# Sparse attention from a written list of steps, shifted copies in one transfer, two squares summed on the matrix engine

## The chip, the cores and the metric

One core of a Trainium2 chip runs the whole program. The metric is device time in microseconds (us) of one execution; the kernel before has a median of 1078.66 us over 3 runs (1078.24 to 1082.45). The engines are PE (matrix engine; PEld is its weight load), DVE (VectorE), ACT (ScalarE), POOL (GpSimd) and SP, which issues the weight loads. Each runs its own instructions in their order and waits on semaphores.

## What is computed

The input is 256 rows of 1024 channels in float32. A first block (mLSTM and window attention, cross attention, feed-forward) is followed by two layers: a conformer convolution with feed-forward, and a sparse attention (NSA) with feed-forward. Three parts of it matter here, cut from the reference:

```python
# every norm: the row's mean square
y = xf * rsqrt(mean(xf * xf, axis=-1) + eps)
# conformer: depthwise convolution over time, 31 taps, on u = a * sigmoid(g)
u[t, c] = sum_j w[j, c] * u[t - 30 + j, c] + b[c]
# NSA, 16 heads of 64 channels, 4 key groups: three branches and a gate for each
o = g[0] * softmax(q k_cmp) v_cmp + g[1] * softmax(q k_slc) v_slc + g[2] * softmax(q k_win) v_win
```

With 256 rows every block is chosen and the window covers all, so the last two branches are plain causal attention, with keys and values of their own.

## The kernel before

Activations lie as 8 tiles of 128 channels x 256 rows. A float32 product is made of three products of float32r halves: each weight chunk of 128x1024 is loaded raw, rounded by ACT (L232, "hi"), its rest taken by DVE (L233, "lo"), and `mm3` (L260 to L262) makes the three products. Weights come through SP in one order for the whole program, four raw chunks ahead.

A norm (`norm`, L478) handles the 8 tiles one by one: DVE adds the residual (L527), ACT rounds (L409), DVE takes the rest (L410), ACT squares (L470), POOL adds the squares of tiles 0 to 6 into one tile (`rowsums`, L500 and L503), and PE multiplies that tile and the last square with ones (L508) into the bank `zb`. Meanwhile PE makes the first product of the next layer, step by step behind the tiles. There are six such sums; four of them have this form.

The conformer (L1050) adds named steps to a `Plan`, each with an engine, an assumed length and what it needs; `Plan.run` puts the steps in order of assumed time and that order is fixed for PE, DVE, ACT and POOL. The first 16 or 20 taps of the convolution are done by PE: for each of 8 tiles, step `w` (L1150) writes the padded rows to DRAM (`cz`), step `c` (L1158) reads them back four times, shifted by 0 to 3 rows, into four groups of 32 partitions (`crp`), in four transfers; step `t` (L1167) multiplies it with the taps in tiles of 32 columns, four beside each other. All of these transfers are issued by POOL, in order; `c` waits until the write of `w` has landed. The other taps are done by DVE (L1197). When all 8 tiles are done, PE sums them and their squares (L1243), the statistics follow (L1255 and on), and the projection starts.

Sparse attention (L1379) is a set of generators: each unit (a projection, an attention unit of one head pair and branch, a finish) yields between its parts, `NSA_AT` has a time for each, and `timed` emits the parts in that order; from there the compiler's scheduler orders each engine. An attention unit (16 of them) makes scores (L1592, L1595; 64 rows, two heads beside each other), maxima (DVE, L819), exponentials (ACT, L1603, L1605), transposes the probabilities (L827 to L829, copied out by ACT, L831), and multiplies them with the values: `out[queries, 64] = pT^T v`, six products (L1620 to L1622). DVE scales the result by gate and denominator (L1627), POOL adds the two branches (L1633), PE adds the compressed branch (L1642, DVE L1644), and the sum is transposed back (L1648) and split into hi and lo (L414, L415) for the output projection. The rotations (L1448 to L1453) are done by DVE.

Of the kernel before, what the change touches and what calls it, by code (L numbers as in the profile page):

```python
# [9 lines left out]
F32 = mybir.dt.float32  # L10
# [3 lines left out]
ALU = mybir.AluOpType  # L14
# [31 lines left out]
NSA_AT = [  # L46
# [46 lines left out]
class Plan:  # L93
# [9 lines left out]
    def add(self, name, eng, us, fn, need=(), rank=0, at=0.0, lag=0.0):  # L103

        self.names[name] = len(self.steps)
        self.steps.append((name, eng, us, fn, list(need), rank, at, lag))

    def run(self):
        free = dict.fromkeys(self.ENGINES, 0.0)
        done, left, order = {}, list(range(len(self.steps))), []  # L110
        while left:
            best = None
            for i in left:
                name, eng, us, fn, need, rank, at, lag = self.steps[i]
                if any(n not in done for n in need):
                    continue
                t = max([at, free[eng]] + [done[n] + ((0.11 if eng == "dv" else 0.0) if self.steps[self.names[n]][1] == eng else 0.15)
                                           for n in need])
                if best is None or (t, rank, i) < best[0:3]:
                    best = (t, rank, i)  # L120
            t, _, i = best
            name, eng, us, fn, need, rank, at, lag = self.steps[i]
            free[eng] = t + us
            done[name] = t + us + lag
            left.remove(i)
            order.append((t, i))
        self.order = sorted(order)
        with self.tc.manual_schedule(engines={e for e in self.ENGINES.values() if e}):
            for _, i in self.order:
                self.steps[i][3]()  # L130


class Net:
# [70 lines left out]
    def parts(self):  # L204

        while True:
            self.run_ahead(stop=self.coming())
# [282 lines left out]
    def rowsums(self, n):  # L490

        def run():
            acc = None
            for m in range(n - 1):
                sq = yield
                if m == 0:
# [9 lines left out]
            for tt in range(NT):  # L506
                for src in (acc, sq):
# [316 lines left out]
    def pT3(self, p):  # L824
# [228 lines left out]
    def conformer(self, first, pool):  # L1053
# [54 lines left out]
        for m in range(KT):  # L1108
# [43 lines left out]
            @step(f"c{m}", "gp", 2.3 if m < NREP else 2.9, [f"w{m}"] + ([f"t{m - NREP}"] if m >= NREP else []), 0, lag=3.5)  # L1152
            def _(m=m):
# [225 lines left out]
    def nsa(self, first, pool):  # L1379
# [25 lines left out]
        have = set()  # L1405

        def need(*keys):
            while not have.issuperset(keys):
                yield
# [5 lines left out]
        def vals(c, put, key):  # L1415
            b = self.lin2A(self.chunk("n_in", c), xx)
            yield
            for tt in range(NT):
                nc.scalar.mul(put(tt), b[tt].rearrange("p (g d) -> p g d", g=4), rc[:, tt : tt + 1])
            have.add(key)  # L1420
            yield

        def heads(c, gi, dst, key):

            b = b0 if ("n_in", c) in FIRST else self.lin2A(self.chunk("n_in", c), xx)
            yield
            b4 = [t.rearrange("p (h d) -> p h d", h=4) for t in b]
            sq = pool.tile([P, NT, 4, dh], F32, name="nsq", tag="nsq", bufs=1)
            for tt in range(NT):
                nc.scalar.activation(sq[:, tt], b4[tt], AF.Square)  # L1430
            ss = pool.tile([P, NT, 4], F32, name="nss", tag="nss", bufs=2)
            nc.vector.tensor_reduce(ss, sq, axis=AX.X, op=ALU.add)

            nc.vector.tensor_scalar(ss, ss, 1.0 / dh, None, op0=ALU.mult)
            nc.vector.tensor_tensor(ss, ss, r2.unsqueeze(2).to_broadcast([P, NT, 4]), op=ALU.add)
            rs = self.rsqrt(ss.rearrange("p t h -> p (t h)"), NT * 4, "h").rearrange("p (t h) -> p t h", t=2)
            yield
            y = pool.tile([P, NT, 4, dh], F32, name="ny", tag="ny", bufs=2)
            for tt in range(NT):
                nc.vector.tensor_tensor(y[:, tt], b4[tt], rs[:, tt].unsqueeze(2).to_broadcast([P, 4, dh]), op=ALU.mult)  # L1440
            z = kvc[:, :, :, 0:dh] if dst is None else y
            nc.vector.tensor_tensor(z.rearrange("p t h d -> p (t h) d"), y.rearrange("p t h d -> p (t h) d"),
                                    gain[:, gi, :].unsqueeze(1).to_broadcast([P, 8, dh]), op=ALU.mult)
            rt = pool.tile([P, 4, NT, 4, 8], F32, name="rot", tag="rot", bufs=2)
            cos = self.cs[:, :, 0, :].unsqueeze(2).to_broadcast([P, NT, 4, 8])
            sin = self.cs[:, :, 1, :].unsqueeze(2).to_broadcast([P, NT, 4, 8])
            x1, x2 = z[:, :, :, 0:8], z[:, :, :, 8:16]
            nc.vector.tensor_tensor(rt[:, 0], x1, cos, op=ALU.mult)  # L1448
            nc.vector.tensor_tensor(rt[:, 1], x2, sin, op=ALU.mult)
            nc.vector.tensor_tensor(rt[:, 2], x2, cos, op=ALU.mult)  # L1450
            nc.vector.tensor_tensor(rt[:, 3], x1, sin, op=ALU.mult)
            nc.vector.tensor_tensor(x1, rt[:, 0], rt[:, 1], op=ALU.subtract)
            nc.vector.tensor_tensor(x2, rt[:, 2], rt[:, 3], op=ALU.add)  # L1453
            if dst is None:
                have.add(key)
            yield
            if dst is not None:
                have.add(key)
                yf = y.rearrange("p t h d -> p t (h d)")
                tposes([(yf[:, 0, i * P : i * P + P], yf[:, 1, i * P : i * P + P]) for i in range(2)], dst)  # L1460
                yield

        def tposes(srcs, dst):
# [4 lines left out]
            nc.scalar.copy(dst, bt[:, 0 : len(srcs) * S])  # L1468
# [14 lines left out]
        def compress():  # L1483
            yield from need("kc", "vc")
            for g in range(0, G, 2):
                tposes([(kvc[:, 0, g + i, :], kvc[:, 1, g + i, :]) for i in range(2)], kvT[:, g : g + 2, :])
            yield
            bh = self.bank("bh")
            for hf in range(2):
                w1 = [r.rearrange("p (l e) -> p l e", l=8) for r in self.chunk("cmp_w1", hf)]  # L1490
                for i in range(16):
                    l = 16 * hf + i

                    nc.tensor.matmul(bh[:, 0:75].rearrange("p (g n) -> p g n", g=5), w1[i // 8][:, i % 8, :],  # L1494
                                     kvT[:, :, l : l + 225 : 16], start=(l == 0), stop=(l == 31))
            hb = pool.tile([P, 1], F32, name="hb")
            hx = pool.tile([P, 60], F32, name="hx")
            nc.vector.tensor_scalar(hb, bh[:, 60:61], self.col("b1", 0), None, op0=ALU.add)
            nc.vector.tensor_scalar(hx, bh[:, 0:60], hb, None, op0=ALU.add)
            yield  # L1500
            h2 = pool.tile([P, 60], F32, name="h2")
            gp = nc.gpsimd
            gp.tensor_tensor(h2, hx, hx, op=ALU.mult)
# [386 lines left out]
```

## Time and profile before

| | |
|---|---|
| median of 3 runs | 1078.66 us |
| profiled execution, its own time | 1083.75 us |
| its span, first to last instruction | 1082.0 us |
| PE busy, DVE busy, ACT busy, POOL busy | 98%, 73%, 56%, 12% of the span |
| mean granted clock of PE | 0.990 |
| sparse attention | about 737 to 887 us |
| conformer convolution, to its statistics | about 441 to 512 us |

Busy time of PE is not work at its peak: matmuls overlap, so a matmul shown with 0.28 us may start 0.12 us after the one before. For PE the distance from one start to the next is read. A float32 matmul that is not split stands as two records, so a count of 4 is two instructions. In the groups, "idle before" is the engine's idle time ahead of the instruction, with what ended it. The granted clock has two levels, shown as 1.0 (2.4 GHz) and 0.5 (1.2 GHz).

### The profile page before, as it was taken

What the parts mean: (1) busy time and instruction counts of PE and PEld (TensorE: products, weight loads), DVE (VectorE), ACT (ScalarE), POOL (GpSimd) and SP (SyncE); (2) the same over time, 40 slices, a digit from 0 to 9 for tenths busy, and PEclk for the clock granted to TensorE, in tenths of its full rate; (3) what the DMA queues carried; (4) which work ended last, traced back from release to release, by engine and by line L of the source; (5) the groups of instructions that cost most, each with busy time, mean ns of one, the idle gap of its engine ahead of it and who ended that gap; (6) DMA issues with size and microseconds to landing.
All of it is one profiled execution on the core that took longest, in us unless ns stands there. A gap on an engine that the chain in (4) does not pass through costs nothing.

```text
span 1082.0 us, 19870 instructions
## 1 busy us (share of the span) xinstructions
PE 1062.6 (98%) x7550; PEld 973.2 (90%) x7550; DVE 786.7 (73%) x1645; ACT 604.2 (56%) x1134; POOL 127.5 (12%) x335
## 2 busy tenths in 40 slices
PE   9999999999999999998999999999999999999998
PEld 8999999999999988984988888889998998888887
DVE  5886667757888865687988778665668657777763
ACT  7675556556666644422766666444466755666530
POOL 1020003002000000334030000013332112000000
PEclk8999999999999999998999999999999999999999
DMA  8654444434555665486555556655073035556670
GB/s 260 214 168 144 143 132 156 156 118 157 194 195 185 206 182 171 145 213 178 186 190 187 189 185 211 191 183 160 27 223 109 2 118 173 185 190 188 184 210 20
DMA packets 54711, 179.34 MB, mean 166 GB/s; under 512 B 9176, under 2 KB 11096, under 8 KB 54616
## 3 DMA queue, kind: packets, MB, share of 16 engines
q1 hardware_dynamic: 52056, 170.14, 49.5%
q0 software_dynamic: 2560, 7.95, 2.8%
q8 instruction: 59, 0.97, 0.4%
q14 instruction: 36, 0.29, 0.1%
HBM read 175.88 MB, written 2.17 MB: 165 GB/s over the span
## 4 chain that ended last, share of the span: by engine, by line
PE 84%; DVE 5%; DMA 5%; POOL 2%; ACT 2%; issue 2%; SPq 0%; ACTq 0%; POOLq 0%
PE pb L268 29%; PE pb L269 15%; PE pb L260 10%; PE pb L261 10%; PE pb L262 10%; DMA cz<-cuz 3%; POOL crp L1158 1%; DVE wpr L233 1%; DVE xx L410 1%; ACT wpr L232 1%; PE bh L1494 1%; DVE xres L527 1%; PE bt L1167 1%; PE pb L317 1%; DMA wraw<-in_n_out_dram 1%
## 5 line engine op out<-in xcount | busy, mean ns | idle before, releaser
L233 DVE TENSOR_TENSOR wpr<-wraw,wpr 128x1024 fp32r<-128x1024 f32 (+1 forms) x300 | 361.4, 1208 | 161.3 <-ACT wpr L232 159.0
L232 ACT CAST wpr<-wraw 128x1024 fp32r<-128x1024 f32 (+1 forms) x300 | 309.3, 1034 | 190.9 <-PE pb L269 98.0
L268 PE MATMUL pb<-xx,wpr 128*128 128x512 f32 x840 | 294.1, 393 | 0.0
L269 PE MATMUL pb<-xx,wpr 128*128 128x256 f32 x840 | 235.4, 280 | 0.0
L268 PEld LDWEIGHTS pb<-xx,wpr 128*128 128x128 f32 x840 | 158.4, 189 | 33.9
L268 PE MATMUL pb<-fhs,wpr 128*128 128x512 f32 x528 | 186.0, 394 | 0.0
L269 PEld LDWEIGHTS pb<-xx,wpr 128*128 128x128 f32 x840 | 158.5, 189 | 0.0
L269 PE MATMUL pb<-fhs,wpr 128*128 128x256 f32 x528 | 147.3, 279 | 0.0
L260 PE MATMUL pb<-xx,wpr 128*128 128x256 f32 x456 | 130.8, 288 | 0.0
L261 PE MATMUL pb<-xx,wpr 128*128 128x256 f32 x456 | 130.2, 286 | 0.0
L262 PE MATMUL pb<-xx,wpr 128*128 128x256 f32 x456 | 129.3, 284 | 0.0
L268 PEld LDWEIGHTS pb<-fhs,wpr 128*128 128x128 f32 x528 | 99.0, 187 | 23.1
L269 PEld LDWEIGHTS pb<-fhs,wpr 128*128 128x128 f32 x528 | 99.0, 187 | 0.0
L260 PEld LDWEIGHTS pb<-xx,wpr 128*128 128x128 f32 x456 | 87.4, 192 | 1.4
L261 PEld LDWEIGHTS pb<-xx,wpr 128*128 128x128 f32 x456 | 87.8, 193 | 0.9
L262 PEld LDWEIGHTS pb<-xx,wpr 128*128 128x128 f32 x456 | 87.7, 192 | 0.0
L260 PE MATMUL pb<-yy,wpr 128*128 128x256 f32 x256 | 72.8, 284 | 0.7 <-ACT yy L1306 0.7
L261 PE MATMUL pb<-yy,wpr 128*128 128x256 f32 x256 | 71.9, 281 | 0.4 <-DVE yy L1310 0.4
L262 PE MATMUL pb<-yy,wpr 128*128 128x256 f32 x256 | 71.8, 281 | 0.0
L992 ACT COPY ft<-pb 128x256 f32<-128x256 f32 x105 | 38.7, 369 | 54.9 <-PE pb L269 54.9
L260 PE MATMUL pb<-wpr,xx 128*128 128x256 f32 x176 | 50.4, 286 | 0.0
L261 PE MATMUL pb<-wpr,xx 128*128 128x256 f32 x176 | 49.8, 283 | 0.0
(442 smaller groups left out, 1954.7 us busy)
## 6 DMA issues: line engine op xcount, KB each, us to landing
wraw<-in_up_dram SPq DMA_DIRECT2D x44, 512.0 KB, 4.4
wraw<-in_up2a_dram SPq DMA_DIRECT2D x44, 512.0 KB, 4.4
wraw<-in_up2b_dram SPq DMA_DIRECT2D x44, 512.0 KB, 4.1
wraw<-in_w_in_dram SPq DMA_DIRECT2D x22, 512.0 KB, 4.8
wraw<-in_n_in_dram SPq DMA_DIRECT2D x20, 512.0 KB, 4.2
wraw<-in_wkv_dram SPq DMA_DIRECT2D x16, 512.0 KB, 4.5
wraw<-in_dn_dram SPq DMA_DIRECT2D x16, 512.0 KB, 4.3
wraw<-in_c_in_dram SPq DMA_DIRECT2D x16, 512.0 KB, 4.3
```

The lines of the kernel that those rows point to most:

```text
L232: self.nc.scalar.copy(both[:, 0, :], raw)
L233: return lambda: self.nc.vector.tensor_tensor(both[:, 1, :], raw, both[:, 0, :].bitcast(F32), op=ALU.subtract)
L260: mm(out, left[:, 0], right[:, 0], start=start, stop=False, skip_group_check=True)
L261: mm(out, left[:, 0], right[:, 1], start=False, stop=False, skip_group_check=True)
L262: mm(out, left[:, 1], right[:, 0], start=False, stop=stop, skip_group_check=True)
L268: mm(out, left[:, 0], right, start=start, stop=False, skip_group_check=True)
L269: mm(out[:, 0], left[:, 1], right[:, 0], start=False, stop=stop, skip_group_check=True)
L317: mm(b[i][:, 0:S], w[k][:, lo, i * P : i * P + P], self.xx[:, k, ro], start=(k == 0 and lo + ro == 0), stop=(k == KT - 1 and lo == 1), ski ...
L410: nc.vector.scalar_tensor_tensor(lo, src, g, hi.bitcast(F32), op0=ALU.mult, op1=ALU.subtract)
L527: self.nc.vector.tensor_tensor(self.x[:, m, :], acc[m // 2][:, (m % 2) * S : (m % 2) * S + S], self.x[:, m, :], op=ALU.add)
L992: nc.scalar.copy(t, b[:, 1])
L1158: nc.gpsimd.dma_start(r[32 * s : 32 * s + 32, :, 0 : ZW - 3], bass.AP(tensor=z.tensor, offset=s, ap=[[ZW, 32], [32 * ZW, 4], [1, ZW - 3]]))
```

## The change

1. Conformer: `w` lays the four channel blocks of a row group side by side in DRAM, so that one transfer of 128 partitions reads all four shifts. `c` issues one transfer in place of four.
2. Row sums: POOL adds the squares of tiles 0 to 5 only; PE multiplies that tile and the last two squares with ones.
3. Sparse attention: units become steps of a `Plan`, with a list of offsets (`NSA_TURN`) and with counted buffers (`take`, `free`). DVE forms gate over denominator (`d`), the probabilities are scaled before they are transposed (`x`: POOL in 15 units, DVE in the last), and the product is turned round: `out[64 channels, queries] = v^T pT`, both branches and the compressed one into one bank, two heads into the two column halves. Scaling of the result, POOL's addition, DVE's addition and the transposition back go. The order of the projections changes, and the rotations stay on DVE (`NSA_ROT` is empty).

```diff
@@ class Plan
+    def run(self, turn={}, **rooms):
...
+                t = max([at, clock[eng]] + [sorted(rooms[kind])[n - 1] for kind, n in take] +
+                        [done[n] + ((0.11 if eng == "dv" else 0.0) if self.steps[self.names[n]][1] == eng else 0.15)
+                         for n in need])
+                key = (round(t + turn.get(name, 0.0), 6), rank, i)
...
@@ def rowsums
-                if m == 0:
+                if m == n - 2:
+                    late = sq
+                elif m == 0:
...
-                for src in (acc, sq):
+                for src in (acc, late, sq):
...
@@ def conformer
-                nc.gpsimd.dma_start(zs[m % NREP], uz[:, m, :])
+                z = zs[m % NREP]
+                nc.gpsimd.dma_start(bass.AP(tensor=z.tensor, offset=0, ap=[[ZW, 4], [4 * ZW, 32], [1, ZW]]), uz[:, m, :])
...
-                for s in range(4):
-                    nc.gpsimd.dma_start(r[32 * s : 32 * s + 32, :, 0 : ZW - 3],
-                                        bass.AP(tensor=z.tensor, offset=s, ap=[[ZW, 32], [32 * ZW, 4], [1, ZW - 3]]))
+                n = 4 * ZW - 3
+                nc.gpsimd.dma_start(r.rearrange("p j t -> p (j t)")[:, 0:n],
+                                    bass.AP(tensor=z.tensor, offset=0, ap=[[1, 4], [4 * ZW, 32], [1, n]]))
@@ def nsa
+NSA_IN = ["k1", "q0", "v0", "vc", "kc", "q1", "cmp", "v1", "q2", "q3"]
+NSA_ROT = []
+NSA_SCALE = [f"{p}.{b}" for p in range(8) for b in range(2) if (p, b) != (7, 1)]
+NST, NPT = 3, 10
...
+            @step("d" + u, "dv", 0.6, ["e" + u, "gd"], 0 + 0.01 * n)
...
+                nc.vector.reciprocal(den, den)
+                nc.vector.tensor_tensor(d3[:, :, 0:2], den[:, 1, :].unsqueeze(2).to_broadcast([P, 2, 2]),
+                                        gt[:, 1, o : o + 2].unsqueeze(2).to_broadcast([P, 2, 2]), op=ALU.mult)
+                nc.vector.tensor_tensor(d3[:, :, 2], den[:, 0, :], gt[:, 0, o : o + 2], op=ALU.mult)
...
+                s4 = st.rearrange("p s (b k) -> p s b k", b=3)
+                on.tensor_tensor(s4, s4, d3.unsqueeze(3).to_broadcast([P, 2, 3, P]), op=ALU.mult)
...
+            @step(f"F{p}", "pe", 1.95, [f"c{p // 2}", f"C{p}.0", f"C{p}.1", "Vv0", "Vv1"], 1, take=(("bo", 1),),
+                  free=(("pT", 4),))
+            def _():
+                got[f"bo{p}"] = bo = self.bank("bo")
+                for br in range(2):
+                    for kk, c, o in ((0, slice(0, S), slice(0, S)), (1, slice(S, 384), slice(P, S))):
+                        for s in range(2):
+                            g = 2 * (p // 4) + s
+                            nc.tensor.matmul(bo[64 * s : 64 * s + 64, o], vv[:, br, kk, g * dh : g * dh + dh],
+                                             got[f"pT{p}.{br}"][s][:, c], start=(br == 0 and kk == 0), stop=False,
+                                             skip_group_check=True)
+                kr = slice(64 * (p % 2), 64 * (p % 2) + 64)
+                nc.tensor.matmul(bo[:, 0:S], vc[kr, p // 4].rearrange("p s d -> p (s d)"), pcT[kr, p // 2, :],
+                                 start=False, stop=True, skip_group_check=True)
...
+        plan.run(NSA_TURN, sh=2, bt=2, bo=1, bc=1, st=NST, pT=NPT, nsq=1, ny=2, csc=2)
```

## Rows read from the trace of the kernel before

**Rows 1.** page, busy us (share of the span) and instructions of each engine

```profile
PE 1062.6 (98%) x7550; PEld 973.2 (90%) x7550; DVE 786.7 (73%) x1645; ACT 604.2 (56%) x1134; POOL 127.5 (12%) x335
```

**Rows 2.** table of stretches: length, busy of PE, PEld, DVE, ACT, POOL; clock, DMA

```profile
737.00:887.00 150.00, 148.29 (x1245) 140.58 (x1245) 97.44 (x363) 86.43 (x239) 38.98 (x127) 1.00 0.33 104
441.00:518.00 77.00, 72.23 (x638) 57.71 (x636) 61.77 (x171) 28.02 (x60) 31.23 (x68) 0.96 0.67 187
248.50:252.50 4.00, 4.00 (x23) 4.00 (x23) 2.42 (x4) 1.04 (x1) 2.59 (x7) 0.57 0.66 214
```

**Rows 3.** timeline of PE, products and convolution tiles (32 columns)

```profile
456.96 7.07 PE L1120 MATMUL pb<-cxg,wraw 128*128 128x256 f32 x32
...
487.64 5.39 PE L1167 MATMUL bt<-crp,cwd 128*32 128x256 f32 x96
...
496.71 2.37 PE L1167 MATMUL bt<-crp,cwd 128*32 128x256 f32 x40 [0.67 <-DMA crp<-cz]
502.38 4.50 PE L1167 MATMUL bt<-crp,cwd 128*32 128x256 f32 x40 [3.30 <-DMA crp<-cz]
```

**Rows 4.** timeline of PE, row sums of one norm

```profile
247.09 0.38 PE L508 MATMUL zb<-ones,sqa 128*128 128x1 f32 x2 [0.99 <-POOL sqa L503]
```

**Rows 5.** timeline of PE, one attention unit: start, us, line, tile, count

```profile
778.43 0.70 PE L1592 MATMUL bs<-nkT,nqT 64*128 64x256 f32 x4
...
779.28 0.43 PE L1620 MATMUL bo<-nvv,pT 128*128 128x64 f32 x2
...
780.67 0.28 PE L1466 MATMUL bt<-ident,nkvc 128*128 128x128 f32 x1
```

**Rows 6.** timeline of PE, compressed branch and last transpositions

```profile
858.80 0.71 PE L1642 MATMUL bc<-vc,pcT 64*128 64x128 f32 x4
859.44 0.43 PE L1620 MATMUL bo<-nvv,pT 128*128 128x64 f32 x2
...
860.92 0.72 PE L1642 MATMUL bc<-vc,pcT 64*128 64x128 f32 x8
...
864.47 0.61 PE L1648 MATMUL bt<-ident,ntp 128*128 128x128 f32 x4
```

**Rows 7.** groups of POOL by shape: count, busy us, mean ns

```profile
L1633 POOL TENSOR_TENSOR ntp<-ntp,ntw 128x256 f32<-128x256 f32 x8 | 5.9, 737 | 43.3 <-DVE nmx L1599 31.9 <-DVE ntw L1627 11.4
```

**Rows 8.** timeline of POOL, same norm

```profile
245.99 1.05 POOL L503 TENSOR_TENSOR sqa<-sqa,sq 128x256 f32<-128x256 f32 x1 [0.61 <-ACT sq L470]
```

**Rows 9.** groups of ACT in sparse attention: busy us, mean ns

```profile
L1603 ACT ACTIVATE nst<-nst,nmx 128x256 f32<-128x256 f32 x32 | 16.2, 506 | 15.2 <-DVE nmx L1599 15.2
L831 ACT COPY pT<-bt 128x384 f32<-128x384 f32 x32 | 13.6, 485 | 3.6 <-PE bt L829 2.8 <-PE bo L1622 0.8
```

**Rows 10.** DMA issues: queue, count, KB each, median us to landing

```profile
crp<-cz POOLq DMA_DIRECT2D x32, 136.0 KB, 4.0
cwd<-in_c_dw_dram POOLq DMA_DIRECT2D x4, 320.0 KB, 6.0
cz<-cuz POOLq DMA_DIRECT2D x8, 137.5 KB, 5.2
```

**Rows 11.** timeline of POOL, shifted copies: issue time, count, idle before

```profile
497.22 2.21 POOL L1158 DMA_DIRECT2D crp<-cz  x4 [4.33 <-DMA cz<-cuz]
```

**Rows 12.** timeline of DVE, end of the convolution taps

```profile
490.09 0.41 DVE L1143 SCALAR_TENSOR_TENSOR cuz<-cag 128x256 f32<-128x256 f32 x1
...
501.19 0.45 DVE L1197 SCALAR_TENSOR_TENSOR cy<-cuz,par,cy 128x231 f32<-128x231 f32 x1
506.93 0.42 DVE L1210 TENSOR_TENSOR cy<-bt,cy 128x256 f32<-128x256 f32 x1 [5.29 <-PE bt L1167]
```

**Rows 13.** timeline of PE, where the convolution's statistics close

```profile
512.41 0.58 PE L1255 MATMUL zb<-csel,czs 128*128 128x2 f32 x4 [0.56 <-ACT czs L1249]
```

**Rows 14.** timeline of DVE, same norm

```profile
240.04 0.47 DVE L410 SCALAR_TENSOR_TENSOR xx<-xres,par,xx 128x256 fp32r<-128x256 f32 x1
...
246.38 1.34 DVE L410 SCALAR_TENSOR_TENSOR xx<-xres,par,xx 128x256 fp32r<-128x256 f32 x2
```

More of the change, by code (lines that the diff above doesn't have):

```diff
@@ L206, in parts @@
         while True:
+            while self.items[self.stream[self.ready][0]][2] is None:
+                self.ready += 1
             self.run_ahead(stop=self.coming())
@@ L1413, in nsa @@
         nc.vector.tensor_scalar(r2, v, RMS_EPS, None, op0=ALU.mult)
[L1415 to L1456, printed above, removed]
-            if dst is not None:
[L1458 to L1461, printed above, removed]
@@ L1463, in tposes, with step @@
-        def tposes(srcs, dst):
+        rh = pool.tile([P, NT], F32, name="rh")
+        nc.vector.tensor_scalar(rh, rc, 0.5, None, op0=ALU.mult)
+        plan = Plan(self.tc)
+        got, pb = {}, {"k0": b0}
+        def step(name, eng, us, need=(), rank=0, **kw):
+            return lambda fn: plan.add(name, eng, us, fn, need, rank, **kw)
+        weights = self.parts()
+        ends, split_at = {}, []
+        for i, (name, idx, k) in enumerate(self.items):
+            if name == "n_in" and i >= self.used:
+                ends[i] = "P" + next(u for u, c in NSA_COL.items() if c == idx)
+            elif name == "cmp_w1":
+                ends[i] = f"bh{idx}"
+            elif name == "n_out":
+                ends[i] = f"o{2 * idx + 1}"
@@ new lines, in nsa, with _ @@
+        last = max(ends) + 2
+        live = [p for p in range(self.ready) if self.stream[p][0] >= self.used]
+        gone, split_of = [], {}
+        p = self.ready
+        held = list(range(self.ready, self.loaded))
+        while self.stream[p][0] <= last:
+            i, j = self.stream[p]
+            if p >= self.loaded:
+                old = p - NRAW
+                oi = self.stream[old][0]
+                @step(f"ld{p}", "sp", 1.3, [f"lo{old}" if self.items[oi][2] else ends[oi]] + ([f"ld{p - 1}"] if p > self.loaded else []),
+                      lag=2.6)
+                def _():
+                    self.run_ahead(stop=self.coming())
+            if self.items[i][2] is not None:
+                live.append(p)
+                old = live[-1 - NHI] if len(live) > NHI else None
+                late = [ends[self.stream[old][0]]] if old is not None else []
+                ld = [f"ld{p}"] if p >= self.loaded else []
+                @step(f"hi{p}", "ac", 0.96, late + ld + ([f"lo{live[-2]}"] if len(live) > 1 and live[-2] >= self.ready else []), 6)
+                def _():
+                    next(weights)
+                @step(f"lo{p}", "dv", 1.15, [f"hi{p}"], 6)
+                def _():
+                    next(weights)
+                split_of.setdefault(i, []).append(f"lo{p}")
+            p += 1
@@ new lines, in product, with _, vals @@
+        def product(u, prev, take=(("sh", 1),)):
+            i = next(i for i, e in ends.items() if e == "P" + u)
+            @step("P" + u, "pe", 5.75, split_of.get(i, []) + prev, 5, take=take)
+            def _():
+                pb[u] = self.lin2A(self.chunk("n_in", NSA_COL[u], stop=self.coming()), xx)
+        def vals(u, put):
+            @step("V" + u, "ac", 0.8, ["P" + u], 2, at=5.0, free=(("sh", 1),))
+            def _():
+                for tt in range(NT):
+                    nc.scalar.mul(put(tt), pb[u][tt].rearrange("p (g d) -> p g d", g=4), rc[:, tt : tt + 1])
@@ L1483, in compress @@
         def compress():
[L1484 to L1488, printed above, removed]
-            for hf in range(2):
[L1490 to L1495, printed above, removed]
+            @step("ct", "pe", 0.95, ["rkc", "Vvc"], 1, take=(("bt", 2),))
@@ new lines, in _ @@
+            def _():
+                got["ct"] = [tposes([(kvc[:, 0, g + i, :], kvc[:, 1, g + i, :]) for i in range(2)])
+                             for g in range(0, G, 2)]
+            @step("cc", "ac", 1.05, ["ct"], 1, free=(("bt", 2),))
+            def _():
+                for g in range(0, G, 2):
+                    nc.scalar.copy(kvT[:, g : g + 2, :], got["ct"][g // 2][:, 0:512])
+            for hf in range(2):
+                @step(f"bh{hf}", "pe", 4.3, ["cc", "Pq1"] if hf == 0 else ["bh0"], 0, take=(("bc", 1),) if hf == 0 else (),
+                      at=0.0)
+                def _(hf=hf):
+                    if hf == 0:
+                        got["bh"] = self.bank("bh")
+                    w1 = [r.rearrange("p (l e) -> p l e", l=8) for r in self.chunk("cmp_w1", hf, stop=self.coming())]
+                    for i in range(16):
+                        l = 16 * hf + i
+                        nc.tensor.matmul(got["bh"][:, 0:75].rearrange("p (g n) -> p g n", g=5), w1[i // 8][:, i % 8, :],
+                                         kvT[:, :, l : l + 225 : 16], start=(l == 0), stop=(l == 31))
@@ new lines, in _ @@
+            @step("ht", "ac", 0.25, ["h2"], 0)
+            def _():
+                nc.scalar.activation(h2, h2, AF.Tanh, scale=math.sqrt(2.0 / math.pi))
+            @step("hg", "gp", 3.0, ["ht"], 0)
+            def _():
+                gp.tensor_scalar(h2, h2, 0.5, 0.5, op0=ALU.mult, op1=ALU.add)
+                gp.tensor_tensor(h2, h2, hx, op=ALU.mult)
+                for c in range(4):
+                    gp.tensor_copy(gT[:, :, c, 0:15], h2.rearrange("p (g n) -> p g n", g=4))
+            @step("kk", "pe", 1.4, ["hg"], 0, take=(("bc", 1), ("bo", 1)))
@@ new lines, in _ @@
+            def _():
+                got["bk"], got["bv"] = bk, bv = self.bank("bk"), self.bank("bv")
+                for g in range(G):
+                    s = g % 2
+                    nc.tensor.matmul(bk[64 * s : 64 * s + 64, (g // 2) * 16 : (g // 2) * 16 + 16], w2[0:64, :],
+                                     gT[0:64, g, 0, 0:16], start=True, stop=True)
+                for g in range(G):
+                    nc.tensor.matmul(bv[:, g * dh : g * dh + dh], gT[64:128, g].rearrange("p c n -> p (c n)"), w2[64:128, :],
+                                     start=True, stop=True)
@@ L1662, in nsa, with _ @@
-        accs = []
-        timed([(u[0], u[1], kinds[u[2]](*u[3:])) for u in NSA_AT])
+            @step("Pg", "pe", 2.85, ["Pq0"], 4, take=(("sh", 1),))
+            def _():
+                got["bg"] = bg = self.bank("bg")
+                for k in range(KT):
+                    self.mm3(bg[0:48, 0:S], wgp[:, k], xx[:, k], k == 0, k == KT - 1)
+            @step("gs", "ac", 0.4, ["Pg"], 2, free=(("sh", 1),))
+            def _():
+                nc.scalar.copy(gs, got["bg"][0:48, 0:S])
+            @step("gT", "pe", 0.3, ["gs"], 1, take=(("bt", 1),))
@@ new lines, in nsa, with _ @@
+        gates()
+        compress()
+        for c in range(4):
+            cmp_branch(c)
+        for p in range(8):
+            for br in range(2):
+                attend(p, br, 2 * p + br)
+            finish(p)
+        accs = []
+        prod = self.proj_steps("n_out", accs, lambda k: ())
+        for k in range(KT):
+            parts = [l for i, e in ends.items() if e == f"o{k | 1}" for l in split_of.get(i, [])]
+            @step(f"o{k}", "pe", 2.85, [f"L{k}"] + parts + ([f"o{k - 1}"] if k else []), 3, take=(("sh", 4),) if k == 0 else ())
+            def _():
+                next(prod)
@@ L1664, in nsa @@
+        plan.run(NSA_TURN, sh=2, bt=2, bo=1, bc=1, st=NST, pT=NPT, nsq=1, ny=2, csc=2)
+        if PLAN_LOG is not None:
+            PLAN_LOG.extend((round(t, 2), *plan.steps[i][0:3], "nsa") for t, i in plan.order)
         return accs
```

404 lines of the change are left out of this document (222 added, 182 removed), and 23 rows, old and new, of tables (NSA_AT, NSA_TURN).

## The prediction

> **What bounds the kernel now.** I read the page first: PE is busy for 98% of the span, DVE for 73%, ACT for 56%, POOL for 12% [rows 1]. A busy PE isn't PE at its peak, so next came the table of stretches and PE's timeline, start to start. In sparse attention (737 to 887 us) PE is busy for 148.29 of 150 us at full clock, while DVE has 97.4 us, ACT 86.4 and POOL 39.0 [rows 2]: what counts there is how many matmuls PE issues, and the holes are small. In the conformer stretch (441 to 518) PE has 72.2 of 77 us and a mean clock of 0.96 [rows 2]. There the chain of waits leaves PE for POOL and the transfers, and PE's timeline shows why: 3.30 us of idleness ahead of the tile at 502.38, until a shifted copy landed, and then a tile of 4.50 us where the one before took 2.37 [rows 3]. The clock had fallen to its lower level after the idleness. The third place is the end of four norms, where PE waits 0.99 us for POOL's addition [rows 4]; behind two of them the clock falls too, to 0.57 over 4 us, so about 3.4 us at the lower level, of which half, 1.7, is lost [rows 2].
>
> **Sparse attention, PE.** One attention unit multiplies probabilities and values from 779.28 to 780.67, 1.39 us [rows 5]; 16 units make 22.2 us. The compressed branch takes 0.64 us per finish (858.80 to 859.44), two finishes beside each other about the same (the row with a count of 8) [rows 6]; I take seven such pieces for the eight finishes, 4.5 us. The transpositions back, four in 0.61 us of overlapping records [rows 6], are two per finish: some 0.2 us each, 1.6 us in all. Removed: 28.3 us.
>
> Added are eight steps `F`, each with eight products of 64 columns (four with 256 rows streaming, four with 128) and the compressed product with 256. No row shows 64-column tiles, so I bound them. In the convolution four instructions on four 32-column tiles, 256 rows streaming, cost 0.45 us together (5.39 us for 96 records, that is 48 instructions, 12 such fours), while one instruction on the whole array with the same 256 rows costs 0.44 (7.07 us for 32 records, 16 instructions) [rows 3]. Column tiles run beside each other there; if two 64-column halves do too, a pair costs 0.45 or 0.22. `F` is then 2 x 0.45 + 2 x 0.22 = 1.34, plus 0.44, plus three changes of tile shape. A change costs about 0.1 us: the six product instructions that follow scores take 1.39, and by two in 0.43 [rows 5] 1.29. With 0.3 for three, F is 2.1 us and eight are 16.7. If the halves don't overlap, F is 4 x 0.45 + 4 x 0.22 + 0.74 = 3.4, and eight are 27.3. So PE loses 11.6 us of work, or 1.0 at the other end; I take 11.6, the convolution's tiles being the nearest row. Scores and first transpositions stay.
>
> **What hides the rest.** DVE loses 24 evacuations of 128x256 and gains the small `d`. POOL gets `x`, 128x768: its row is 0.737 us for 128x256 [rows 7], so 0.74 at least (if length didn't matter) and 2.2 by three times that; where DVE was working beside it, an addition took 1.05 [rows 8], which makes 3.2. I take 2.2; fifteen of them are 33 us of POOL's time, on an engine that idles for 111 of 150 us. It is hidden while PE has other work, but it lies in each unit's chain: maxima, exponentials, `d`, `x`, transposition. ACT spends at least (16.2 + 13.6) / 16 = 1.9 us per unit on the first exponentials and the copies alone [rows 9], so near the end, when the projections are gone and the units of the last two projections are left, ACT and POOL deliver more slowly than PE takes. Before, PE's longer products filled part of that. I put 2.5 us of new holes there; from below, holes could shrink by the 1.7 us that PE idles now, and from above they end in the third rival. Behind a late `x` stand, on POOL, the reciprocal roots of later projections; behind a late transposition stand, on PE in its written order, the products. The steps' weight splits are the same in number. Sparse attention: -11.6 + 2.5 = -9.1 us (-13.5 to the rival's +14).
>
> **Conformer.** POOL's queue is a chain: `w` is issued, lands (5.2 us [rows 10]), then four copies are issued in 2.21 us, 0.55 each, then the next `w`; ahead of the copies POOL idled 4.33 us for a landing [rows 11]. With one copy a round is 1.66 us shorter, over seven rounds 11.6 us, more than POOL is behind: the last `w` comes after 499.43, where its data are ready at 490.5 [rows 12]. What is late next is the data. From 490.5: `w` and its landing, 5.2 from issue, 495.7; `c` 0.3 later; its landing. One copy of 549 KB isn't in the trace: between the 4.0 us of a quarter (136 KB) and, at four times the bytes, 16 if time went by bytes; a transfer of 320 KB takes 6.0 [rows 10], so bytes count for little: 2.0 us for 184 KB more, by which 549 KB is an estimated 8.5. Four quarters issued together from 497.22 moved the same bytes, and the tile that waited for the last of them began 5.2 us later, at 502.38 [rows 3, 11]. I take 5.5, and 8.5 for the second rival. That is 501.5; the tile takes 2.3, addition, square and sum 1.5: 505.3. DVE had finished its taps at 501.6 but for about 2.5 us of work that stood behind the late tile [rows 12], so it ends by 504.1 at the earliest and doesn't stop this. Before, the sums closed at 511.9 (512.41 less the idle 0.56) [rows 13]. Gain 6.5 us, of which 2.1 is the tile at the lower clock; 3 to 1 if the copy takes 7 us or more and PE waits again, 8 if PE and DVE run dense.
>
> The Trainium skill, "DMA: Bandwidth & Descriptors", section on the anatomy of a DMA issued by GpSimd, fits 2.0 us plus bytes by 436 GB/s; by it the copy would land in an estimated 3.3 us and the second rival would fall away. It gives an estimated 2.8 for 320 KB, and the row shows 6.0, so the measurement decides and the rival stays.
>
> **Row sums.** Each of six sums gets two more matmul instructions of one column on PE: four records in a beat of 0.11, 0.44 us, 2.6 in all. Two sums lie in dense PE work and cost their 0.9. In the four others POOL's last addition goes: it ran from 245.99 to 247.04 [rows 8], and PE went on at 247.09 [rows 4]. But the next products wait for DVE's rest of tile 6, the first of the pair from 246.38 (1.34 us for two, against 0.47 for one while POOL was idle) [rows 14], so at about 247.0 too. What is late next is DVE, a little earlier than now because POOL leaves it alone; the added matmuls fit into the hole. I take -0.5 for each of the four, between +0.2 (hole stays, work added) and -1.0, and nothing for the clock, which fell behind two of the four [rows 2]. Sum: +0.9 - 2.0 = -1.1 (-3.1 to +1.7).
>
> **Sum.** -9.1 - 6.5 - 1.1 = -16.7 us. Against the profiled execution, 1083.75, that is 1067.0. The median is 5.1 us lower, 1078.66; taken off there it is 1062.0. Some of the time at the lower clock (2.1 in the convolution) may be missing in a faster execution, so I put 1 us back: 1063.
>
> **Rivals.**
> First, the 64-column halves don't run beside each other. For it: no such row. Against: four 32-column tiles do. Sparse attention is then -1.0 + 2.5, the total -6.1: 1072.5.
>
> Second, the single copy lands so late that PE waits in the convolution as before, the queue only being emptied sooner. For it: landings of 4 to 6 us for less data [rows 10], with the DMA engines at 0.67 of their time in this stretch [rows 2]. Then the convolution gains 1 in place of 6.5: 1068.
>
> Third, slower: POOL becomes the queue that everything in sparse attention waits for. The norm shows DVE and POOL slowing each other, 0.47 to 0.67 for DVE, 0.74 to 1.05 for POOL [rows 7, 8, 14]. If `x` takes 3.2 us (48 us for fifteen), DVE waits out most of it, and its 97 us, less 10 for the evacuations, plus 48, plus some 28 us in which POOL's reciprocal roots and DVE block each other, become 163, where PE's stretch was 149. That is +14, -6.5 and -1.1 stay: +6.4, 1085. It decides from an `x` of about 2.9 us on if every one collides. Against: DVE's reads from PSUM make up much of its work and are not seen to slow down. The Trainium skill, "GPSIMD Engine Reference", Key points, says that GpSimd shares its SBUF interfaces with VectorE, with contention where a VectorE instruction has two SBUF inputs, and is about half as fast on elementwise work; the norm's rows agree with the contention (0.67 for 0.47).
>
> Fourth, it goes better: no new holes (-13.5), the convolution dense (-8), the norms' clock kept (-3): -24.5, 1054.
>
> **How the numbers follow.** Forecast 0.53, first rival 0.10, second 0.13, third 0.11, fourth 0.13. 0.5%, 5.4 us, is about what a measurement of this kernel can tell from no change. The forecast, the second and fourth rivals and half of the first are faster by more than that, 0.84, less 0.04 for mixtures of small gains with late projections: 0.80; same 0.09; slower 0.11. The forecast's own range is 1057 to 1069. The range of eight in ten takes in the second rival and most of the fourth, and reaches past the first's 1072.5: 1052 to 1074.
>
> **What would show it.** In the profile after: an `F` from first to last matmul of about 2.1 us (3.4: first rival); sparse attention some 140 us long, PE at full clock in it; PE's holes between the last projection and the output projection; `x` near 2.2 us on POOL; no idleness of PE ahead of the seventh convolution tile, no lower clock there, and the statistics closing 6.5 us sooner after the stage's start; the wait ahead of the row sums at half its 0.99 us, ended by DVE. I am wrong if sparse attention isn't 6 us shorter, or if the gain comes from elsewhere.

## The result, and the profile after

Slower: 1117.89 us (1116.83 to 1120.29, 3 runs) against 1078.66; ratio 1.0343, interval 1.0316 to 1.037. I had forecast 1063, 1052 to 1074. The profiled execution after is that of 1117.89 us, its span 1116.1 (before: 1083.75 and 1082.0), so the two profiles differ by 34.1 us; the rest of the 39 is that the profiled execution of before was 5 us above its median.

The page first: engines' busy time, PE's busy time and granted clock in 40 slices of 27.9 us, and the issues of the two transfers (from the table of transfers: KB each, median us to landing).

```profile
PE 1061.9 (95%) x7478; PEld 961.5 (86%) x7478; DVE 791.9 (71%) x1638; ACT 603.7 (54%) x1134; POOL 129.0 (12%) x312
PE   9999999999999999873699999999999899999998
...
PEclk8999999999999999996799999999999999999999
...
crp<-cz POOLq DMA_DIRECT2D x8, 548.5 KB, 12.2
...
cz<-cuz POOLq DMA_DIRECT2D x8, 137.5 KB, 11.0
```

PE is as busy as in [rows 1], but spread over 34 us more. Slices 17 to 20 (446 to 558 us) hold the loss, the last two of them at a lower clock; and in [rows 10] the write `w` landed in 5.2 us and a copy of a quarter in 4.0. PE's waits in the conformer (us in total, times, longest), and the row that closes the statistics:

```profile
PE bt L1194 <- DMA crp<-cz: 38.1, 6, 11.1
...
550.51 0.58 PE L1282 MATMUL zb<-csel,czs 128*128 128x2 f32 x4 [0.55 <-ACT czs L1276]
```

The statistics close 38.1 us later than in [rows 13]; before, PE waited for copies for 0.67 and 3.30 us [rows 3]. POOL's timeline shows the round: the copy, the write of the next tile, a transfer of tap weights (`cwd`), then over 10 us of waiting for that write's landing.

```profile
497.88 0.67 POOL L1185 DMA_DIRECT2D crp<-cz  x1 [13.10 <-DMA cz<-cuz]
498.54 0.71 POOL L1177 DMA_DIRECT2D cz<-cuz  x1
499.23 0.60 POOL L1102 DMA_DIRECT2D cwd<-in_c_dw_dram  x1
510.17 0.70 POOL L1185 DMA_DIRECT2D crp<-cz  x1 [10.34 <-DMA cz<-cuz]
```

Why does it land so late? The table of stretches (length; busy of PE, PEld, DVE, ACT, POOL; clock; DMA share; GB/s) for 3 us in the middle of that copy:

```profile
505.00:508.00 3.00, 0.00 (x0) 0.00 (x0) 0.00 (x0) 0.00 (x0) 0.00 (x0) 0.50 0.27 78
```

for 2 us of before with four quarters and the next write in flight:

```profile
499.20:501.20 2.00, 0.00 (x0) 0.00 (x0) 2.00 (x7) 0.42 (x1) 1.34 (x3) 1.00 0.92 240
```

In the first stretch nothing computes, the clock has fallen, and the DMA engines are busy for 0.27 of their time, 4.3 of 16; in before it was 0.92. The trace's transfer records say the same: of the copy's 128 packets of 4388 B four are in flight at a time (0.28 us each, 32 in a row: 9 us), beside 384 packets of 4 B.

The write behind it shares its fate. Its data, 32 packets of 4400 B, ran from 499.9 to 502.6. But 96 packets of 16 B go with each such write (none in before), and of these 64 were through by 500.3 and the last 32 ran only from 507.5 to 508.7, when the copy's last packets ended. POOL went on at 510.17; in all six such rounds it did so 0.8 to 1.5 us after the last of these packets. The tap weights, issued after both, show it too: 48 of their 64 packets had ended by 504.1, the other 16 ran from 507.6 to 509.9. So each transfer behind the copy had packets that ran only when the copy was done.

### The profile page after: what moved, and what is told of

It is laid out like the page before. It is cut to its first block, busy times and chain, and to the rows that moved or that the text cites. A ratio compares the mean times of both kernels' runs of the same rounds, so it can differ in the third digit from the quotient of the medians.

```text
span 1116.1 us, 19664 instructions
## 1 busy us (share of the span) xinstructions
PE 1061.9 (95%) x7478; PEld 961.5 (86%) x7478; DVE 791.9 (71%) x1638; ACT 603.7 (54%) x1134; POOL 129.0 (12%) x312
## 4 chain that ended last, share of the span: by engine, by line
PE 85%; DMA 5%; issue 4%; DVE 3%; ACT 1%; POOL 1%; SPq 0%; POOLq 0%; ACTq 0%
PE pb L291 28%; PE pb L292 14%; PE pb L283 11%; PE pb L284 11%; PE pb L285 10%; DMA cz<-cuz 3%; DMA crp<-cz 1%; PE bs L1736 1%; PE bt L1785 1%; PE bo L1804 1%; PE bh L1597 1%; PE zb L533 1%; PE pb L340 1%; DVE wpr L256 0%; DMA wraw<-in_up2a_dram 0%
## 5 line engine op out<-in xcount | busy, mean ns | idle before, releaser
L1194 PE MATMUL bt<-crp,cwd 128*32 128x256 f32 x288 | 24.6, 506 | 38.1 <-DMA crp<-cz 38.1
L1194 PEld LDWEIGHTS bt<-crp,cwd 128*32 128x32 f32 x288 | 12.3, 141 | 49.8 <-issue 43.8
```

Of the source, the lines that this page charges most:

```text
L1194: nc.tensor.matmul(bt[m][c, 0:S], wd[m][:, i, c], reps[m % NREP][:, j, PAD - 4 * i : PAD - 4 * i + S], start=(i == 0), stop=(i == CONV_G[m ...
```

## The experiments

Ratios are to the kernel before on the same chip, with a 95% interval in brackets; us are medians.

**e1: before, with the new `w` and `c` alone.**

```diff
-                nc.gpsimd.dma_start(zs[m % NREP], uz[:, m, :])
+                nc.gpsimd.dma_start(<z as [[ZW, 4], [4 * ZW, 32], [1, ZW]]>, uz[:, m, :])
...
+                <r> = <z as [[1, 4], [4 * ZW, 32], [1, 4 * ZW - 3]]>   # one transfer for four
```

> Before with the conformer's w and c of the change, nothing else. Theory A: the whole loss sits in these two transfers, because the count in the outermost place of their DRAM pattern (4) decides how many of the 16 DMA engines carry them: the profile of the changed kernel has 4 packets of 4388 B in flight at a time, and the convolution closes 40 us later. Then this kernel takes 1115 to 1121 us. Rival: the loss needs the rest of the change too (sparse attention's list or its other weight order takes the queues): clearly less, 1080 to 1105 us.

Measured: 1121.02 us, 1.0353 (1.0314 to 1.0393). The whole loss is here.

**e2: the changed kernel, with `w` and `c` of before** (e1's diff, reversed).

> The changed kernel with the conformer's w and c of before. What is left is sparse attention and the row sums. By the differences of the two profiles (row sums -2.4 up to 250 us, +1.1 at two later norms, sparse attention -4.2) it is some 6 us below before's profiled execution, 1072 to 1075 us against the median. By my forecast's terms it would be -10.2: 1068. Rival: the executions of before that were timed had no need of these gains (the profiled one was the slowest of four): 1077 to 1079.

Measured: 1077.87, 0.9966 (0.9952 to 0.9979): 3.7 us of gain, less than either forecast of mine; the rival's range holds it, but before had 1081.84 on this chip.

**e3: the changed kernel, `c` with 32 outermost.**

```diff
-  <r> = <z as [[1, 4], [4 * ZW, 32], [1, n]]>
+  <r> = <z as [[4 * ZW, 32], [1, 4], [1, n]]>    # partition 4 * row + shift
-    A["c_dw"] = dw.reshape(P, KT, 8, P)
+    A["c_dw"] = dw.transpose(1, 0, 2, 3, 4, 5).reshape(P, KT, 8, P)
```

> The changed kernel with the same bytes in the same rows of 4388 B, in one transfer, but the DRAM pattern of c has 32 in the outermost place and the four shifts in the second; the partitions' order and that of the tap weights follow. w stays as in the change (outermost 4). Theory A: c lands in 4 to 6 us instead of 12.2, 16 packets in flight; the convolution closes at or before the time it had in before: 1068 to 1077 us. Rival B (one transfer of 549 KB, or rows of an odd length, is slow by itself): c still lands in 10 us or more, 1105 to 1120 us.

Measured: 1078.2, 0.9964 (0.9946 to 0.9982). Same bytes, same rows, same single transfer, and it lands in half the time (table of transfers, a stretch in which only this copy moves data, and POOL's timeline):

```profile
crp<-cz POOLq DMA_DIRECT2D x8, 548.5 KB, 6.0
cz<-cuz POOLq DMA_DIRECT2D x8, 137.5 KB, 6.8
...
496.20:497.80 1.60, 0.00 (x0) 0.00 (x0) 1.60 (x6) 0.09 (x1) 0.38 (x1) 1.00 0.89 277
...
478.90 0.54 POOL L1184 DMA_DIRECT2D crp<-cz  x1 [7.87 <-DMA cz<-cuz]
479.42 0.74 POOL L1177 DMA_DIRECT2D cz<-cuz  x1
480.16 0.56 POOL L1102 DMA_DIRECT2D cwd<-in_c_dw_dram  x1
486.62 0.53 POOL L1184 DMA_DIRECT2D crp<-cz  x1 [5.89 <-DMA cz<-cuz]
```

So the order of the pattern's counts is the cause, not the size or the odd length of a row. But it is no faster than e2, and PE still waits 3.41 and 2.82 us for its last two copies: the round is still 7.7 us, 5.9 of it waiting for the write, although the 1.66 us of issue are gone as expected.

**e4: the changed kernel with its `w`, and four copies.**

```diff
-  <r> = <z as [[1, 4], [4 * ZW, 32], [1, n]]>
+  for s in range(4):  <r[32 * s : 32 * s + 32]> = <z + s as [[4 * ZW, 32], [1, n]]>
```

> The changed kernel with w of the change (outermost 4) and c again in four transfers, each with 32 outermost and rows of 4388 B. It prices w alone. Theory A: w's 32 packets of 4400 B go 4 at a time, 8 in a row of 0.26 us each, 2.1 us instead of 0.6, so w lands 1.5 us later than before (6.5 to 7 us for 5.2), and the total is 0 to 6 us above e2. Rival: w's 11.0 us were its own: 8 rounds of 5 us more, 25 us or more above e2.

Measured: 1080.33, 0.9987 (0.9974 to 1.0001); `w` landed in 5.2 us, as in before and not in the 6.5 to 7 that I had expected. So a `w` with 4 outermost costs little by itself; in the change it was late because the copy was ahead of it. Whether the 2 us to e2 are real stays open, the intervals overlap.

**e5 and e6: the next tile's write ahead of this tile's copy**, in e3 and in e2:

```diff
-  @step(f"c{m}", "gp", ..., [f"w{m}"] + ...
+  @step(f"c{m}", "gp", ..., [f"w{m}"] + ([f"w{m + 1}"] if m < KT - 1 else []) + ...
```

> e3 with one thing more: POOL issues the write w of the next tile ahead of the copy c of this one (c gets the next w as a need); the orders of PE and the bytes stay. In e3 a copy landed in 6.0 us, near my 5.5, and yet the convolution closed no sooner than with four copies, with PE waiting 3.41 and 2.82 us. Theory D: a round is bound by the write's landing, which POOL waits out with the next write behind it (w 6.8 + c's issue 0.54 + w's 0.74 = 8.1 us a round in e3, w 5.1 + 2.18 + 0.56 = 7.8 with four copies), so fewer issues buy nothing; with the next write ahead, the last copy starts when its data are there. Then PE's two waits shrink to under 2 us together, the convolution closes 3 to 5 us sooner than in e3: 0.991 to 0.994 of before. Rival: DVE's taps or the copy's own landing set the end; the time stays at e3's 0.9964 within 0.15%.

> e2 (four copies and w as before) with the same order: next w ahead of this tile's copies. Theory D: it gains 3 to 5 us on e2 as well, 0.992 to 0.995 of before; beside e5 it tells what one transfer is worth once the order is mended (by issue time alone, 1.66 us once at the end). Rival (the number of issues is what counts): no gain here and a gain in e5.

Measured: 1073.28, 0.9929 (0.9911 to 0.9947), and 1073.25, 0.9936 (0.9919 to 0.9953). Each is some 0.3% below the kernel that it changes, with intervals that just touch. The profiles are clearer. From the first product that PE does for the taps (454.85 us in e3, 453.10 in e5) to the row that closes the statistics, e3 takes 56.1 us and e5 50.0; e2 takes 57.0 and e6 50.2. The closing rows of e3 and e5:

```profile
510.98 0.58 PE L1281 MATMUL zb<-csel,czs 128*128 128x2 f32 x4 [0.55 <-ACT czs L1275]
```

```profile
503.06 0.58 PE L1281 MATMUL zb<-csel,czs 128*128 128x2 f32 x4 [0.55 <-ACT czs L1275]
```

One transfer or four makes no difference that these runs can tell. POOL's timeline of e5: from the fourth write to the eighth it now waits for DVE's data; only its first and its last copy still wait for a landing.

```profile
471.90 0.72 POOL L1177 DMA_DIRECT2D cz<-cuz  x1 [6.94 <-DVE cuz L1168]
472.62 0.58 POOL L1184 DMA_DIRECT2D crp<-cz  x1
478.98 0.71 POOL L1177 DMA_DIRECT2D cz<-cuz  x1 [5.78 <-DVE cuz L1168]
```

**e7 and e11: all scalings of the probabilities on DVE**, in e2 as steps of DVE, by which `Plan.run` lays out a new order with the old offsets (e7), in e5 in the old places (e11):

```diff
-NSA_SCALE = [f"{p}.{b}" for p in range(8) for b in range(2) if (p, b) != (7, 1)]
+NSA_SCALE = []                                                                   # e7
-                on.tensor_tensor(s4, s4, d3...)
+                nc.vector.tensor_tensor(s4, s4, d3...)                           # e11
```

> e2 with all 16 scalings of the probabilities on DVE (the changed kernel has 15 on POOL, 1.47 us each, and one on DVE, 0.95 us). Theory L: while POOL runs one of them, a DVE instruction that starts beside it lasts until it ends (1.38 for 0.69 us, 1.37 for 0.22, 1.46 for 0.15 in the profile of the changed kernel), so each costs DVE about 1.1 us anyway; on DVE they cost 0.95 and no wait between engines: time within 2 us of e2's, or below it, 0.993 to 0.998 of before. Rival (POOL relieves DVE, the holes of PE are DVE's load): DVE gets 14 us more in a stretch where it is already busy for 108 of 150 us, and PE waits for part of it: 4 to 10 us above e2, 1.000 to 1.006 of before.

> e5 with all scalings of the probabilities issued to DVE (0.95 us each), but in the places that the written order gave them on POOL: e7 changed the order too. Theory of load: e7's 18 us above e2 are DVE's own time (15 x 0.95 = 14 us in the stretch where PE waits for DVE), so this is as slow: 1.008 to 1.014 of before. Rival, the order: e7's list was laid out anew for it and badly; with the old order it is within 5 us of e5: 0.993 to 0.998.

Measured: e7 1096.16, 1.0144 (1.0129 to 1.0159), beyond both expectations; e11 1073.41, 0.9917 (0.9891 to 0.9942), near the rival's range. The same instructions on DVE make the kernel 1.7% slower than e2 in a new order, and no slower than e5 in the old one: e7's 18 us go with the order, not with DVE's load.

**e8: before, with the row sums alone** (the diff of `rowsums` above).

> Before with the row sums of the change alone. My forecast had -1.1 us (-3.1 to +1.7). By the two profiles: -2.4 us up to 250 us of the span (the wait ahead of two sums and the lower clock behind one), +1.1 at two later norms, so 0.998 to 1.000 of before. Sparse attention by itself is then e2 less this.

Measured: 1080.5, 0.9996 (0.9983 to 1.001). So the row sums are worth nothing that can be told from this run (by the ratio -0.4 us, -1.8 to +1.1), and sparse attention, e2 less that, some 3 us.

**e9, e10, e13: the chain to q2's transposition**, all from e5: reciprocal roots of q2 and q3 on DVE (e9); their rotations left out (e10); q2's scaling and rotation ahead of the maxima of unit 3.0 (e13).

```diff
-  self.rsqrt(got["ss" + u]..., NT * 4, "h")
+  self.rsqrt(got["ss" + u]..., NT * 4, "h", nc.vector if u in ("q2", "q3") else None)   # e9
+  if u in ("q2", "q3"): return      # e10, first line of step r
+  ahead=[("yq2", "m3.0"), ("rq2", "m3.0")]      # e13, moves in the written order
```

> e5 with the reciprocal roots of the last two projections (q2, q3) on DVE (8 small instructions of some 0.2 us, 1.6 us) in place of POOL's 13 in a row (3.9 to 4.4 us); every step's place in the written order stays. In the changed kernel and in e5 PE runs dry when the projections are done: it waits 1.6 and 0.67 us for q2 to be normed, rotated and transposed, and then the clock stands at the lower level for 7 to 10 us, which costs half of that. Theory C (sparse attention gives back its gain there: the chain square, sum, root, scale, rotate of the last two projections): the chain is some 2 us shorter, so the hole shrinks by 1.5 us or more, and if the clock then stays up another 3.5 to 5 us go: 0.986 to 0.990 of before (e5 had 0.9929). Rival (the loss is spread over many small waits, or DVE is the bound there and is only loaded more): 0.992 to 0.996.

> e5 without the rotations of q2 and q3 (six DVE instructions each, 1.35 us alone, 2.5 us beside POOL's scaling; this part of the computation is left out). Theory C: the chain to q2's transposition is 1.35 us shorter and q3's 1.35 to 2.5, the hole of 1.6 us almost closes: 1.5 to 3 us less with the clock still falling, 5 to 7 if it stays up: 0.986 to 0.9915 of before. Rival (the rotations' place on DVE is no limit): within 0.1% of e5's 0.9929.

> e5 with one move in DVE's written order: scaling and rotation of q2 stand ahead of the maxima of unit 3.0, which stood ahead of them (1.3 us). e9's roots on DVE only joined DVE's queue, and the hole grew to 2.67 us; e10, with two rotations left out, kept nearly the same idle time of PE (5.8 for 6.2 us) but the clock did not fall, and sparse attention was 4.8 us shorter. Theory H: what costs is the clock's fall behind the hole ahead of q2's transposition (10.2 us at the lower level in e5, 5.1 lost); q2 then comes 1.3 us sooner, the hole of 1.58 us shrinks to 0.3, the clock stays up: 3.5 to 5 us less than e14 beside it, 0.988 to 0.990 of before. Rival: DVE is the bound there and the hole only moves to unit 3.0's transposition, the clock falls all the same: within 1.5 us of e14.

Measured: e9 1073.72, 0.9913 (0.9886 to 0.994), between its two expectations, and beside e5 no difference that can be told; e10 1070.19, 0.989 (0.9861 to 0.9919), as theory C had it; e13 1076.59, 0.9965 (0.9951 to 0.9979), no better than its neighbour e14, as its rival had it. Where PE waits around q2 (PE's timeline), in e5:

```profile
815.85 0.30 PE L1558 MATMUL bt<-ident,ny 128*128 128x128 f32 x1 [1.58 <-DVE nden L1764]
817.21 1.65 PE L1735 MATMUL bs<-nkT,nqT 64*128 64x256 f32 x8 [0.68 <-ACT nqT L1553]
```

in e9:

```profile
815.65 0.44 PE L1558 MATMUL bt<-ident,ny 128*128 128x128 f32 x1 [2.67 <-DVE nden L1764]
```

and in e13:

```profile
815.73 0.30 PE L1562 MATMUL bt<-ident,ny 128*128 128x128 f32 x1 [0.27 <-DVE ny L1547]
820.39 1.65 PE L1739 MATMUL bs<-nkT,nqT 64*128 64x256 f32 x8 [4.04 <-ACT nqT L1557]
```

e9 lengthened the hole of 1.58 us, e13 closed it and opened one of 4.04 behind it, on ACT's copy. Of the three only e10, with less work for DVE (110.9 us in sparse attention for 114.3 in e5), helped. The stretch 810 to 830 us of e5 (length; busy of PE, PEld, DVE, ACT, POOL; clock; DMA share; GB/s):

```profile
810.00:830.00 20.00, 17.74 (x115) 13.11 (x115) 15.22 (x62) 10.43 (x37) 9.56 (x18) 0.74 0.00 1
```

and of e10:

```profile
810.00:830.00 20.00, 18.18 (x155) 13.64 (x156) 16.33 (x75) 14.43 (x53) 11.00 (x19) 1.00 0.00 1
```

PE's busy time is nearly the same, but the clock stood at 1.00 instead of 0.74, which is 10.4 us at the lower level, 5.2 lost; e10's sparse attention was 4.8 us shorter (152.8 for 157.6, from sum of squares to sum of squares). Its size in the medians is less sure, 3.2 us to e11 beside it, with intervals that overlap.

**e14: e5 again; e12 and e15: before, with e5's order of `w`.**

> e5 once more, beside e13 and e15 on one chip: 0.992 to 0.994 of before (e5 had 0.9929). If the gain was one of that day's executions: 0.996 or more.

> Before with one thing changed: POOL issues the write of the next tile ahead of the four copies of this one. Theory D: the convolution's loss in before was this order and nothing of the change is needed for it; PE's 3.30 us ahead of the seventh tile go with the lower clock behind it: 3 to 5 us, 0.9955 to 0.997 of before. Rival (it needs the other parts of the change): 0.999 to 1.001.

> e12 once more, since its interval (0.997 to 1.0014) holds both answers. Theory D: its convolution closed 3.9 us sooner in its profile, so 0.996 to 0.9975 of before. Rival: what the convolution gains there is lost behind it, where PE waits 1.32 and 1.02 us for the normed tiles in place of 0.66 and 0.35 and the clock falls for another 3.4 us: 0.9985 to 1.000.

Measured: e14 1075.64, 0.9951 (0.9934 to 0.9968), between its two expectations; e12 1081.38, 0.9992 (0.997 to 1.0014); e15 1078.85, 0.9988 (0.9977 to 1.0). The mended change (e5 and e14: `c` with 32 outermost, the next write ahead) is 0.5 to 0.7% faster than before. The order alone gives the kernel before 0.1%, with intervals that reach 1, not the 0.3% that it gave e2. From the first product for the taps to the close of the statistics, before takes 55.5 us, e12 53.1 and e15 52.7 (so 2.4 and 2.8 sooner, not 3.9), against the 6.8 us that e6 gains on e2: one wait of 3.0 and 2.6 us for a copy is left in e12 and e15. Behind the statistics PE waits 1.3 and 1.0 us in place of 0.66 and 0.35, but it does so in e6 too. Why e2 gains more is open.

## Why the prediction was wrong

**The step that failed is the conformer's landing**: "I take 5.5, and 8.5 for the second rival". I had bounded it by bytes and by four quarters in flight together, and the order of the counts in the pattern was not among the bounds. A copy of 549 KB lands in 11.6 to 12.2 us with 4 in the outermost place of its DRAM pattern (e1 and the change) and in 6.0 with 32 (e3), so 5.5 was near for a pattern that the change does not have. -6.5 became about +40 (38.1 against [rows 13], and 2.2 that had been gained before the convolution). Of these, 34 are PE's waits for copies (38.1 for 4.0); most of the rest is tiles at the lower clock, 3.9 to 4.5 us for 2.4, four of them where before had one. The second rival, a copy that lands late, had the mechanism and stopped at "as before": the lower clock in and behind the four longest waits, and the write of the next tile behind the copy, were not in it.

The Trainium skill, "DMA: Bandwidth & Descriptors", section on why a DMA counts by 16, says how many engines a transfer uses: the largest number up to 16 that divides the slowest dimension (of those above 1) of both patterns. By that, 4 for the change and 16 for e3 and before. The runs agree: 0.27 of the DMA engines' time for the change, 0.89 for e3 and 0.92 for before. I cited this page for its line of bytes only; the diff showed the `[1, 4]` in front.

**"Over seven rounds 11.6 us, more than POOL is behind" and "What is late next is the data" failed too.** In e3 a copy landed in 6.0 us, near the forecast, and nothing was gained: POOL waits for the write's landing with the next write unissued behind the wait, and that landing grew from 5.2 to 6.8 us as the issues shrank. The round was bound by what stood behind a wait in a queue, which e5 and e6 show by changing only that (6.1 and 6.8 us of the convolution in the profiles).

**Sparse attention's work was sized right, its holes were not.** `F` in the changed kernel (PE's timeline):

```profile
875.61 1.52 PE L1804 MATMUL bo<-npT,nvv 128*64 128x256 f32 x16
877.06 0.70 PE L1808 MATMUL bo<-pcT,vc 64*128 64x256 f32 x2
877.69 0.87 PE L1785 MATMUL bt<-ident,nst 128*128 128x128 f32 x6
```

875.61 to 877.69 is 2.08 us where I had 2.1: column halves run beside each other, and the first rival falls. But from sum of squares to sum of squares the stretch went from 160.62 to 156.49 only. The stretches before and after the change, and below the latter the part of it in which the clock falls:

```profile
734.44:895.06 160.62, 157.93 (x1320) 149.74 (x1319) 107.71 (x383) 94.98 (x258) 44.04 (x133) 1.00 0.33 104
```

```profile
773.08:929.57 156.49, 150.27 (x1229) 135.75 (x1228) 114.33 (x376) 96.05 (x258) 61.72 (x139) 0.98 0.35 109
860.00:871.00 11.00, 9.22 (x55) 7.05 (x55) 9.29 (x40) 4.70 (x15) 4.33 (x7) 0.69 0.01 1
```

PE idles 6.2 us for 2.7, so 3.5 of new holes (I had 2.5), and from 860 to 871 us the clock is 0.69: 6.8 us at the lower level, 3.4 lost, a term that I had for the convolution and the norms and not here. -11.6 + 3.5 + 3.4 = -4.7, near the -4.1 measured; PE's busy time fell by 7.7 us, which with the 3.4 is 11.1 less work for the 11.6 of the forecast. (The best end of my range, -13.5, is -13.3 by its own terms, 11.6 and 1.7.)

DVE is the engine that more than half of the holes wait for. PE's waits in that stretch of the changed kernel:

```profile
PE bt L1718 <- DVE nden L1765: 1.9, 1, 1.9
PE bt L1559 <- DVE nden L1765: 1.6, 1, 1.6
PE bt L1785 <- POOL nst L1777: 1.4, 2, 1.1
PE bs L1736 <- ACT nqT L1554: 1.4, 2, 0.7
```

I had DVE's time fall by 10 us with the evacuations; it rose from 107.7 to 114.3. `x` took 1.59 us on average on POOL (1.47 in most rows), less than my 2.2, but DVE's timeline shows the same two instructions with POOL idle or at small work (first and second row) and beside two scalings (third and fourth), which POOL's timeline has last:

```profile
859.16 0.69 DVE L1530 TENSOR_TENSOR ny<-ny,gain 128x512 f32<-128x512 f32 x1
859.89 0.22 DVE L1539 TENSOR_TENSOR rot<-ny,ang 128x64 f32<-128x64 f32 x1
862.14 1.38 DVE L1530 TENSOR_TENSOR ny<-ny,gain 128x512 f32<-128x512 f32 x1
863.56 1.37 DVE L1539 TENSOR_TENSOR rot<-ny,ang 128x64 f32<-128x64 f32 x1
...
861.50 3.34 POOL L1777 TENSOR_TENSOR nst<-nst,nd 128x768 f32<-128x768 f32 x2 [0.19 <-ACT npT L1791]
```

That is the third rival's mechanism, with scalings of 1.6 us and not 3.2. e11 gives its size: with 15 scalings more on DVE, 14 us of work (15 x 0.95), DVE is busy for 117.4 us in the stretch, 3.1 more than in e5, so beside POOL they had cost DVE some 11 us. That these 11 us made the holes is argued and not shown: in e11 DVE is as loaded without them, and the hole ahead of q2 (1.69 us) and the lower clock behind it stay.

**Row sums**: forecast -1.1, e8 -0.4 with an interval that holds both. In e8's profile the four waits for POOL (4.0 us in before's) are gone, and the two falls of the clock behind norms with them; over all its executions nothing of this can be told.

## What to carry to other kernels

Before merging transfers, read the outermost count of both access patterns: one transfer in place of four ran on a quarter of the engines here, and the DMA share of a quiet stretch shows it at once. When a queue waits for a landing, ask what stands unissued behind the wait; that order was worth more here than the issues saved. And cost a hole of PE with the clock behind it, not by its length.

## What the runs showed of the hardware that I had not expected

- A write of 137.5 KB whose data had gone by 502.6 landed at about 510: 32 of the 96 packets of 16 B that went with it ran only when the copy issued ahead of it was done (508.7).
- Three DVE instructions that take 0.15 to 0.69 us alone took 1.37 to 1.46 us beside POOL's scalings (862.14 and 863.56 above; 885.82, 128x2).
- Holes of 1.57 to 1.61 and 0.67 us, 0.7 us of work apart, were followed by the lower clock for 6.8 to 10.2 us in each of e2, e3, e5, e6 and e14; holes of 0.47 and 1.35 in e10 were not.
